# First feed-forward product by Strassen's scheme on pairs of output blocks, in a two-layer hybrid block with a state-space tail

## The chip, the cores and the metric

The kernel is one program on one core of one Trainium2 chip. The time of a run is the device time of that program in microseconds (us); the table below gives the median of three runs. The engines of the core are TensorE (PE in the profile; its weight loads are a row of their own, PEld), VectorE (DVE), ScalarE (ACT), GpSimd (POOL) and SyncE (SP), which only issues transfers here. Each engine works through its own instructions in the order in which the program puts them, and waits where an instruction needs something that another engine has not yet made.

## The reference, cut to what matters

Two hybrid layers run one after the other, then a second block (state space, pooling, gates). The change concerns the feed-forward part of the two layers. There are 512 tokens, the model width D is 1024 and D_FF is 4096:

```
h2 = rmsnorm(x, pre_mlp_g)
ff = jnp.square(jax.nn.relu(h2 @ w_ff1)) @ w_ff2
return x + rmsnorm(ff, post_mlp_g)
```

The product `h2 @ w_ff1` is (512 x 1024) by (1024 x 4096). All matrices are float32. The other products of a layer, the second block and the tables of its state-space branch (`ssm_*` inputs) are computed as before.

## The kernel before

**Tiles.** Activations stand transposed in SBUF: 128 features on the partitions, 512 tokens along the row; a 1024-wide activation is a list of KD = 8 such blocks. A float32 product is made of three products in a shorter format: each operand is split into a high part and a rest (ScalarE casts the high part, VectorE subtracts it), and `mm3` (L77 to L81) issues three matmuls per block: weight high by input high, weight high by input rest, weight rest by input high. All three have their record at L78 or near it, so nearly all of TensorE's work reads as one line.

**Weights.** `load_w` (L167) fetches one 1024 x 128 block of weights into a `raw` tile (512 KB, issued on SP), ScalarE casts it to `wh` (L183), VectorE makes the rest `wl` (L184). Two `raw` buffers are shared by the whole kernel, a third one (`rawx`) takes every third load in the stages that call `third`; `wh` and `wl` have three buffers each, and a cast into one waits until TensorE has used what lay there.

**Products.** `dense` (L194) makes one output block for all 512 tokens: 8 blocks x 3 = 24 matmuls with 512 columns. `dense_half` (L212) does the same for 256 tokens, with 24 matmuls of 256 columns.

**Feed-forward of a layer.** The 32 output blocks of the first product are made in four groups of eight (`gidx`, loop at L1281), and after each group its contribution to the second product is made and added into `acc`. The first six blocks of group 0 are made by halves of the tokens while the normalisation before them still runs (`NFF = 6`); the last two of group 0 and all of groups 1 to 3 use `dense`, which makes 26 such blocks per layer. Each block goes through `relu2`: three ScalarE steps (`ft`, `fq`, cast to `hh`) and one VectorE step (the rest `hl`). In groups 0 to 2 the second product is `dense` too; in group 3 it is `dense_half`, first with weights that are kept in `kw` tiles.

**What else runs there.** `ssm_tables` (L933) is a generator that prepares constant tables for the second block; each `next(tables, None)` lets it make one step, with small VectorE and GpSimd operations (`cmul`, L915 to L921) and a few transposes on TensorE. A half of the tables is made in each layer, inside this feed-forward part, and before the change it is finished before group 3.

**Order.** A scheduler sets the order of instructions on every engine at build time from the order of the code, the buffers and its own estimates; only marked matmuls are kept in program order. Between the engines there are only waits.

Of the kernel before, what the change touches and what calls it, by code (L numbers as in the profile page):

```python
# [9 lines left out]
F32 = mybir.dt.float32  # L10
# [9 lines left out]
P = 128  # L20
SEQ = 512
# [33 lines left out]
def body(  # L55
# [110 lines left out]

    def load_w(src, kn=KD, n=P, pool_h=False, keep=None):  # L167
        turn[0] += 1
        if turn[0] % 3 == 2 and turn[1] is not None and turn[0] > turn[2]:
            raw = turn[1].tile([P, kn, n], F32, tag="rawx", name="rawx", bufs=1)  # L170
        else:
            raw = wp.tile([P, kn, n], F32, tag="raw", name="raw", bufs=2)
# [29 lines left out]

    def dense_q(w, xs, m=P):
# [8 lines left out]
    def dense_half(w, xs, i):  # L212
# [5 lines left out]
        return ps  # L218

# [713 lines left out]
    def ssm_tables(sp, hf):  # L933
        def tl(name, shape=(P, NG)):
            return sp.tile(list(shape), F32, tag=name, name=name)

        prs = slice(NG * hf, NG * hf + NG)
        grs = slice(2 * NG * hf, 2 * NG * hf + 2 * NG)
        lam = {}
        for nm, src in (("lr", ssm_lam_re_2), ("li", ssm_lam_im_2)):  # L940
            row = tl("row" + nm, (NG, P))
# [10 lines left out]
        bre, bim = tl("bre", (P, NG, 16)), tl("bim", (P, NG, 16))  # L952
# [4 lines left out]
        wre, wni = tl("wre", (P, NG, 9, 16)), tl("wni", (P, NG, 9, 16))  # L957
        for dst, src in ((wre, ssm_c_re_2), (wni, ssm_c_im_2)):
            crow = tl("crow", (P, 2, 2, 64))
            for dup in range(2):  # L960
                DMA.dma_start(out=crow[:, :, dup, :], in_=src[0, grs].rearrange("(q g) c p -> (g c) q p", q=2))
            for q in range(2):
                ps = ps_ax((P, 8, 16))
                T.transpose(ps.rearrange("p g c -> p (g c)"), crow[:, q].rearrange("p a b -> p (a b)"), ident)
                for half in range(2):
                    hs = slice(64 * half, 64 * half + 64)
                    V.tensor_copy(out=dst[hs, 4 * q:4 * q + 4, 0, :], in_=ps[hs, half::2, :])
        V.tensor_scalar(out=wni[:, :, 0, :], in0=wni[:, :, 0, :], scalar1=-1.0, scalar2=None, op0=ALU.mult)
# [27 lines left out]
        s16 = (P, NG, 16)  # L996
        tC, tD = tl("tC", s16), tl("tD", s16)
        ebr, ebi = tl("ebr", (P, NG, 8, 16)), tl("ebi", (P, NG, 8, 16))
        cmul(ebr[:, :, 7, :], ebi[:, :, 7, :], bc(cor, s16), bc(coi, s16), bre, bim, tC)
        for j in range(6, -1, -1):  # L1000
            cmul(ebr[:, :, j, :], ebi[:, :, j, :], bc(are, s16), bc(aim, s16), ebr[:, :, j + 1, :], ebi[:, :, j + 1, :], tD, eng=G)
            yield
        for k in range(1, 9):
# [599 lines left out]
```

## Time and profile before

| | us |
|---|---|
| median of 3 runs | 2311.5 |
| lowest and highest of the three | 2302.97, 2313.52 |
| profiled execution: its own time | 2312.67 |
| profiled execution: span of the trace | 2311.0 |
| PE busy | 2247.2 (97%) |
| DVE busy | 1340.0 (58%) |
| ACT busy | 896.2 (39%) |
| POOL busy | 463.2 (20%) |

The trace is of one execution; 1.7 us of that run lie outside its span. Matmuls are pipelined, so a record of one lasts longer than the distance to the next: what a matmul costs in a stretch is the stretch divided by the matmuls that started in it. The feed-forward part of layer 0 lies from about 618 us to 986 us of the span; the 26 blocks of the first product that use `dense`, and the second product of groups 0 to 2, from 656.0 us to 937.4 us.

### The profile page before, as it was taken

How to read it: one execution, taken by the hardware profiler on the slowest of the kernel's cores; microseconds unless marked ns; L12 is line 12 of the kernel's file. 1: busy time of each engine (PE TensorE's matmuls, PEld its weight loads, DVE VectorE, ACT ScalarE, POOL GpSimd, SP SyncE). 2: the span in 40 equal slices, each digit the busy share in tenths (PEclk: the TensorE clock that was granted, in tenths of full speed). 3: DMA queues.
4: the chain of work that ended last, by engine and by line, in shares of the span. 5: the costliest groups of instructions: out<-in, count | busy, mean ns of one | idle time of the engine just before them, and what ended most of it. 6: DMA issues, size and time to landing. Idle time of an engine off the chain costs nothing. (4 is left out here: it accounts for less than half of the span.)

```text
span 2311.0 us, 35255 instructions
## 1 busy us (share of the span) xinstructions
PE 2247.2 (97%) x13596; PEld 1914.8 (83%) x13596; DVE 1340.0 (58%) x2698; ACT 896.2 (39%) x1624; POOL 463.2 (20%) x567
## 2 busy tenths in 40 slices
PE   8999999999999999989999999999999999889998
PEld 7867788888988888988677888789878889878788
DVE  5579793445676333565797934467653335444645
ACT  4454233333443233444533333335432334424333
POOL 1644320200440000246343201004300002100001
PEclk9999999999999999999999999999999999999999
DMA  5223334565434333341234245655343334554344
GB/s 176 62 70 91 87 88 137 157 203 169 145 100 133 95 114 101 109 119 53 71 83 96 85 128 169 196 176 151 83 137 93 112 107 122 162 158 122 109 130 146
DMA packets 463987, 279.98 MB, mean 121 GB/s; under 512 B 48118, under 2 KB 439628, under 8 KB 463308
## 3 DMA queue, kind: packets, MB, share of 16 engines
q1 hardware_dynamic: 462416, 277.54, 41.4%
q8 instruction: 107, 1.75, 0.3%
q14 instruction: 60, 0.49, 0.1%
q10 hardware_dynamic: 1404, 0.19, 0.1%
HBM read 231.57 MB, written 46.11 MB: 120 GB/s over the span
## 5 line engine op out<-in xcount | busy, mean ns | idle before, releaser
L78 PE MATMUL psm<-xsh,wh 128*128 128x512 f32 (+1 forms) x1520 | 595.5, 392 | 1.0 <-ACT xsh L223 1.0
L78 PE MATMUL psm<-xsl,wh 128*128 128x512 f32 (+1 forms) x1520 | 580.9, 382 | 5.5 <-DVE xsl L226 3.9
L78 PE MATMUL psm<-xsh,wl 128*128 128x512 f32 (+1 forms) x1520 | 580.9, 382 | 0.0
L184 DVE TENSOR_TENSOR wl<-raw,wh 128x1024 fp32r<-128x1024 f32 (+2 forms) x249 | 304.0, 1222 | 205.5 <-ACT wh L183 179.6
L183 ACT CAST wh<-raw 128x1024 fp32r<-128x1024 f32 (+2 forms) x196 | 199.2, 1017 | 500.0 <-PE psm L78 448.7
L78 PEld LDWEIGHTS psm<-xsh,wh 128*128 128x128 f32 x1520 | 288.6, 190 | 61.8 <-issue 9.7
L78 PEld LDWEIGHTS psm<-xsl,wh 128*128 128x128 f32 x1520 | 288.8, 190 | 57.9 <-DVE xsl L226 4.6
L78 PEld LDWEIGHTS psm<-xsh,wl 128*128 128x128 f32 x1520 | 288.0, 190 | 56.4 <-issue 0.3
L257 POOL TENSOR_TENSOR sa<-sa,sq 128x256 f32<-128x256 f32 x54 | 52.5, 973 | 821.5 <-ACT sq L252 537.5
L78 PE MATMUL psm<-hh,wl 128*128 128x512 f32 (+1 forms) x480 | 177.5, 370 | 1.4 <-DVE wl L184 1.3
L78 PE MATMUL psm<-hh,wh 128*128 128x512 f32 (+1 forms) x480 | 176.9, 369 | 0.0
L78 PE MATMUL psm<-hl,wh 128*128 128x512 f32 (+1 forms) x480 | 176.6, 368 | 0.0
L183 ACT CAST wh<-rawx 128x1024 fp32r<-128x1024 f32 (+1 forms) x67 | 67.0, 999 | 164.0 <-PE psm L78 151.7
L184 DVE TENSOR_TENSOR wl<-rawx,wh 128x1024 fp32r<-128x1024 f32 (+1 forms) x67 | 77.6, 1158 | 63.1 <-ACT wh L183 60.6
L78 PEld LDWEIGHTS psm<-hh,wl 128*128 128x128 f32 x480 | 90.5, 188 | 18.5 <-DVE wl L184 3.7
L78 PEld LDWEIGHTS psm<-hl,wh 128*128 128x128 f32 x480 | 90.5, 189 | 15.2
L78 PEld LDWEIGHTS psm<-hh,wh 128*128 128x128 f32 x480 | 90.3, 189 | 14.7 <-issue 0.2
L181 POOL TENSOR_SCALAR wh<-raw 128x1024 fp32r<-128x1024 f32 (+1 forms) x53 | 61.5, 1162 | 156.0 <-PE psm L78 124.8
L78 PE MATMUL psm<-ah,wh 128*128 128x512 f32 x256 | 80.7, 396 | 2.9 <-ACT ah L223 2.7
L1310 DVE TENSOR_TENSOR acc<-psm,acc 128x512 f32<-128x512 f32 x32 | 22.1, 692 | 102.2 <-PE psm L78 102.2
L78 PE MATMUL psm<-bh,wh 128*128 128x512 f32 x256 | 80.0, 394 | 0.0
L78 PE MATMUL psm<-kq,xsh 128*128 128x256 f32 x384 | 72.6, 290 | 0.0
(627 smaller groups left out, 4332.6 us busy)
## 6 DMA issues: line engine op xcount, KB each, us to landing
raw<-in_w_in_dram SPq DMA_DIRECT2D x136, 512.0 KB, 3.9
raw<-in_w_ff_dram SPq DMA_DIRECT2D x86, 512.0 KB, 3.9
rawx<-in_w_ff_dram SPq DMA_DIRECT2D x42, 512.0 KB, 4.0
gate<-dg SPq DMA_DIRECT2D x48, 256.0 KB, 3.8
raw<-in_w_up_sw_dram SPq DMA_DIRECT2D x12, 512.0 KB, 5.0
raw<-in_w_up_dn_dram SPq DMA_DIRECT2D x10, 512.0 KB, 4.9
raw<-in_w_o_dram SPq DMA_DIRECT2D x10, 512.0 KB, 3.6
db<-sof SPq DMA_DIRECT2D x16, 256.0 KB, 3.1
```

The source lines that it names most:

```text
L78: return s.issue(nc.tensor.matmul(*a, **k))
L181: G.tensor_scalar(out=h, in0=raw, scalar1=1.0, scalar2=0.0, op0=ALU.mult, op1=ALU.add)
L183: S.copy(out=h, in_=raw)
L184: V.tensor_tensor(out=lo, in0=raw, in1=f32(h), op=ALU.subtract)
L257: (G if s.n in POOL_ACC else V).tensor_tensor(out=s.acc, in0=s.acc, in1=sq, op=ALU.add)
L1310: V.tensor_tensor(out=acc[n], in0=ps, in1=acc[n], op=ALU.add)
```

## The change

The 26 `dense` blocks of the first product in each layer become 13 pairs. A pair is two neighbouring output blocks for all 512 tokens, that is two 1024 x 128 blocks of weights. Inputs (8 blocks), tokens (two halves `p1`, `p2`) and the two output blocks are the three two-fold splits of Strassen's scheme in Winograd's form: seven products of 4 input blocks by 256 tokens instead of eight. A product is 4 x 3 = 12 matmuls of 256 columns, a pair 84 of them; before, two output blocks were 48 matmuls of 512 columns.

What the scheme needs beside the products: `load_pair` makes the sums of weights on GpSimd (four operations of 128 x 512) and splits 3.5 weight blocks instead of 2 into high part and rest. They are called `d` (the block as loaded), `x`, `y` and the half block `z`, whose tiles `s1`, `sh`, `sl` have one buffer each. `fast_pair` puts the seven products into four PSUM tiles (`psa`), and one ScalarE copy and seven VectorE additions of 128 x 256 make the two outputs `y0` and `y1`. `token_sums` makes the sums of inputs once per layer, while the last half-loop of group 0 runs: it reads the normalised input back from memory (eight loads of 256 KB) and holds the results in `ta` and `tb`.

Around it: four raw buffers, two of them in a pool `wx` of the stage (tag `raws`); `rawx` is not used in the stage until group 3's second product; the hidden tiles have 8 buffers instead of 10; `dense2` starts the second product of groups 0 to 2 with two output blocks together, six input blocks each, before it needs the last pair's outputs; the steps of `ssm_tables` stand in another order, share tiles and are finished after the pairs of group 3, so that its tiles, the token sums and `wx` are released there; the `kw` tiles of group 3's second product lie where they were.

```
+    def dense2(ws, xs):
+        ps = [ps_mm() for _ in ws]
+        kn = len(xs)
+        order = (*range(kn - 2), kn - 1, kn - 2)
+        for ks in (order[:-2], order[-2:]):
+            for p, (h, lo) in zip(ps, ws):
+                for k in ks:
+                    mm3(p, h[:, k, :], lo[:, k, :], *xs[k], k == order[0], k == order[-1])
+        return ps
+    def load_pair(src, c, pool):
+        r0, r1 = raw_tile(), raw_tile()
+        for j, r in enumerate((r0, r1)):
+            DMA.dma_start(out=r, in_=src[:, (c + j) * P:(c + j + 1) * P].rearrange("(k p) n -> p k n", p=P))
+        a1, a2 = slice(0, 4), slice(4, 8)
+        s1 = pool.tile([P, 4, P], F32, tag="s1", name="s1", bufs=1)
...
+            S.copy(out=h, in_=raw)
+            V.tensor_tensor(out=lo, in0=raw, in1=f32(h), op=ALU.subtract)
+            return h, lo
+        d = parts(r0)
+        G.tensor_tensor(out=s1, in0=r1[:, a1], in1=r1[:, a2], op=ALU.add)
+        G.tensor_tensor(out=r1[:, a1], in0=r0[:, a1], in1=r1[:, a1], op=ALU.subtract)
+        x = parts(r1)
+        G.tensor_tensor(out=r0[:, a1], in0=s1, in1=r0[:, a1], op=ALU.subtract)
+        G.tensor_tensor(out=r0[:, a2], in0=r0[:, a2], in1=r0[:, a1], op=ALU.subtract)
+        return d, x, parts(r0), parts(s1)
+    def fast_pair(w, xs, ts):
...
+        for b, c, (h, lo), k0, rhs in ((0, p1, d, 0, b11), (0, p2, d, 4, b21), (1, p1, x, 4, t4), (1, p2, x, 0, t3),
+                                       (2, p1, y, 0, t2_), (2, p2, y, 4, b22), (3, p1, z, 0, t1)):
+            for k, ((rh, rl), rc) in enumerate(rhs):
+                mm3(ps[b][:, c], h[:, k0 + k, :], lo[:, k0 + k, :], rh[:, rc], rl[:, rc], k == 0, k == 3, pin=c is p2 and k == 0)
+        y0, y1 = r2("y0", (P, SEQ)), r2("y1", (P, SEQ))
+        u, v = y0[:, p2], y1[:, p2]
+        S.copy(out=u, in_=ps[0][:, p1])
+        for o, i, a in ((y0[:, p1], ps[0][:, p2], u), (u, ps[2][:, p1], u), (v, ps[1][:, p2], u), (y1[:, p1], ps[1][:, p1], v),
+                        (u, ps[2][:, p2], u), (v, ps[3][:, p1], v), (u, ps[3][:, p1], u)):
+            V.tensor_tensor(out=o, in0=i, in1=a, op=ALU.add)
+        return y0, y1
+    def token_sums(st, pool):
...
+            for t, kk in ((a, k), (b, k + 4)):
+                DMA.dma_start(out=t, in_=st.d[:, kk, :])
+                S.activation(out=t, in_=t, func=AF.Copy, scale=pcol(st.gname, st.g0 + kk))
+            V.tensor_tensor(out=a[:, p1], in0=a[:, p2], in1=a[:, p1], op=ALU.subtract)
+            G.tensor_tensor(out=a[:, p2], in0=b[:, p2], in1=a[:, p2], op=ALU.subtract)
+            V.tensor_tensor(out=b[:, p2], in0=b[:, p2], in1=a[:, p1], op=ALU.subtract)
+            V.tensor_tensor(out=b[:, p1], in0=b[:, p1], in1=b[:, p2], op=ALU.subtract)
...
                 while len(hid) < KD:
-                    c0 = (gidx * KD + len(hid)) * P
-                    ps = dense(load_w(w_ff1[l][:, c0:c0 + P]), mid.xs)
-                    next(tables, None)
-                    hid.append(hidden(0))
-                    relu2(ps, *hid[-1])
+                    ys = fast_pair(load_pair(w_ff1[l], gidx * KD + len(hid), spare[0]), mid.xs, ts)
+                    for _ in range(2):
+                        next(tables, None)
+                        hid.append(hidden(0))
+                    for y, hl in zip(ys[::-1], hid[:-3:-1]):
+                        relu2(y, *hl)
...
                 if gidx < 3:
+                    first = dense2([load_w(wsrc(n)) for n in range(2)], hid)
                     for n in range(KD):
-                        ps = dense(load_w(wsrc(n)), hid)
+                        ps = first[n] if n < 2 else dense(load_w(wsrc(n)), hid)
```

Three places show how the instructions of an engine stand. The first is ScalarE where the half-loop of group 0 ends and the first full-width product of the layer begins, in layer 0. Before the change (`ft`, `fq`, `hh` are the last half block's `relu2`, `dt` a step of the tables, `wh_6935` weights of the second product):

```order
L1254 ACTIVATE ft_6711<-psm_6686 128x256
L1256 ACTIVATE fq_6713<-ft_6711 128x256
L223 CAST hh_6498<-fq_6713 128x256
L971 ACT_TABLE_LOAD
L971 ACTIVATE dt_6777<-dt_6777 128x8
L183 CAST wh_6935<-raw_6933 128x1024
L1254 ACTIVATE ft_6813<-psm_6740 128x512
```

The same place in the changed program (`wh_6822` is `x` of the first pair, `sh_6832` its `z`, `wh_6828` its `y`; `psa_6836` holds the pair's first two products, those with `d`):

```order
L1347 ACTIVATE ft_6786<-psm_6761 128x256
L1349 ACTIVATE fq_6788<-ft_6786 128x256
L307 CAST hh_6501<-fq_6788 128x256
L277 COPY y0_6924<-psa_6836 128x256
L1047 ACT_TABLE_LOAD
L1047 ACTIVATE dt_6946<-dt_6946 128x8
L252 CAST sh_6832<-s1_6815 128x512
L252 CAST wh_6822<-raws_6812 128x1024
L252 CAST wh_6828<-raw_6811 128x1024
```

The cast of `x`, which the pair's third product needs, now stands behind the copy of the pair's own first products, and in layer 0 behind the table load as well. In layer 1 the table load and the cast of `z` stand ahead of the copy, and only the copy ahead of `x`:

```order
L252 CAST sh_16985<-s1_16968 128x512
L1047 ACT_TABLE_LOAD
L1047 ACTIVATE dt_17099<-dt_17099 128x8
L277 COPY y0_17077<-psa_16989 128x256
L252 CAST wh_16975<-raw_16965 128x1024
```

The second place is VectorE between the last block of the first product and group 3's second product, layer 0. Before (`kw_8899` is the rest of the first weight block of that product, `hl_8769` the rest of the sixth hidden block):

```order
L184 TENSOR_TENSOR wl_8779<-rawx_8776,wh_8778 128x1024
L226 TENSOR_TENSOR hl_8691<-fq_8694,hh_8690 128x512
L184 TENSOR_TENSOR kw_8899<-rawx_8896,kw_8898 128x1024
L184 TENSOR_TENSOR wl_8818<-raw_8815,wh_8817 128x1024
L226 TENSOR_TENSOR hl_8730<-fq_8733,hh_8729 128x512
L184 TENSOR_TENSOR wl_8857<-raw_8854,wh_8856 128x1024
L184 TENSOR_TENSOR kw_8933<-raw_8930,kw_8932 128x1024
L226 TENSOR_TENSOR hl_8769<-fq_8772,hh_8768 128x512
```

After (`psa_9661` and `psa_9662` hold the last pair's `y` and `z` products):

```order
L280 TENSOR_TENSOR y1_9748<-psa_9660,y1_9748 128x256
L280 TENSOR_TENSOR y0_9747<-psa_9661,y0_9747 128x256
L280 TENSOR_TENSOR y1_9748<-psa_9662,y1_9748 128x256
L280 TENSOR_TENSOR y0_9747<-psa_9662,y0_9747 128x256
L192 TENSOR_TENSOR kw_9786<-raw_9783,kw_9785 128x1024
L192 TENSOR_TENSOR kw_9820<-raw_9817,kw_9819 128x1024
```

The rest of the first kept weights stood four blocks ahead of its use; it now stands behind the last additions of the pairs, and layer 1 has the same order. The third place is VectorE in group 2 of layer 0, between the first pair's weights and the second's (after the change; `A` and `B` are the tables that `cmul` makes, `wl_8472` is `d` of the second pair, `wl_8478` its `x`):

```order
L1002 TENSOR_TENSOR A_8289<-A_8289,tC_7650 128x8x16
L1003 TENSOR_TENSOR tC_7650<-aim_7056,A_8289 128x128
L1001 TENSOR_TENSOR A_8289<-are_7055,A_8289 128x8x16
L1005 TENSOR_TENSOR B_8290<-B_8290,tC_7650 128x8x16
L253 TENSOR_TENSOR wl_8472<-raw_8466,wh_8471 128x1024
L1000 TENSOR_TENSOR tC_7650<-aim_7056,B_8290 128x128
L280 TENSOR_TENSOR y0_8428<-psa_8340,y0_8428 128x256
L1004 TENSOR_TENSOR B_8290<-are_7055,B_8290 128x8x16
```

These 48 `cmul` steps stood among the first `dense` blocks of group 0 and group 1; they now stand among the pairs of group 2, in both layers.

## Rows read from the trace of the kernel before

**Rows 1.** The page's first part: busy us (share of span) x instructions

```profile
PE 2247.2 (97%) x13596; PEld 1914.8 (83%) x13596; DVE 1340.0 (58%) x2698; ACT 896.2 (39%) x1624; POOL 463.2 (20%) x567
```

**Rows 2.** A PE group, 656.0 to 937.44 us: busy, mean ns | idle before, releaser

```profile
L78 PE MATMUL psm<-xsh,wh 128*128 128x512 f32 x208 | 81.8, 393 | 0.0
```

**Rows 3.** Windows: a half-wide stretch, then full-width first product of group 3

```profile
core 0: us, PE busy (x) PEld busy (x) DVE busy (x) ACT busy (x) POOL busy (x), PEclk, DMA share, GB/s
580.04:594.43 14.39, 14.39 (x122) 14.39 (x121) 6.23 (x12) 4.09 (x7) 1.48 (x2) 1.00 0.34 97
893.92:937.44 43.52, 43.52 (x193) 36.04 (x192) 19.63 (x20) 24.43 (x33) 0.00 (x0) 1.00 0.48 137
```

**Rows 4.** ACT groups of the whole span, by shape

```profile
L183 ACT CAST wh<-raw 128x1024 fp32r<-128x1024 f32 x179 | 187.9, 1050 | 476.9 <-PE psm L78 438.2 <-issue 13.5 <-DVE wl L184 8.8
L1256 ACT ACTIVATE fq<-ft 128x512 f32<-128x512 f32 x52 | 32.9, 632 | 1.4
L223 ACT CAST hh<-fq 128x512 fp32r<-128x512 f32 x52 | 32.2, 620 | 1.6
L1254 ACT ACTIVATE ft<-psm 128x512 f32<-128x512 f32 x52 | 30.7, 591 | 0.0
...
L859 ACT COPY sc<-psa 128x256 f32<-128x256 f32 x48 | 15.3, 371 | 13.3 <-PE psa L78 13.0
```

**Rows 5.** DVE groups of the whole span, by shape

```profile
L184 DVE TENSOR_TENSOR wl<-rawx,wh 128x1024 fp32r<-128x1024 f32 x59 | 72.1, 1221 | 62.4 <-ACT wh L183 60.0 <-PE psm L78 2.4
...
L226 DVE TENSOR_TENSOR hl<-fq,hh 128x512 fp32r<-128x512 f32 x52 | 36.0, 692 | 20.4 <-ACT hh L223 20.4
...
L1324 DVE TENSOR_TENSOR acc<-psm,acc 128x256 f32<-128x256 f32 x32 | 13.3, 421 | 34.6 <-PE psm L78 34.6
...
L921 DVE TENSOR_TENSOR wni<-wni,tC 128x128 f32<-128x128 f32 x16 | 4.9, 308 | 0.1
```

**Rows 6.** POOL groups of the whole span, two inputs, 128x512

```profile
L545 POOL TENSOR_TENSOR tg<-tri,gh 128x512 fp32r<-128x512 f32 x16 | 21.2, 1325 | 6.5 <-ACT gh L487 3.6 <-PE psa L78 2.9
...
L722 POOL TENSOR_TENSOR st<-st,eg 128x512 f32<-128x512 f32 x8 | 8.3, 1040 | 61.8 <-DVE st L747 43.1 <-DVE st L745 18.7
```

**Rows 7.** PE in order of time, end of group 3's first product: start, us

```profile
937.22 0.39 PE L78 MATMUL psm<-xsh,wl 128*128 128x512 f32 x1
937.44 0.28 PE L78 MATMUL psm<-hh,kw 128*128 128x256 f32 x1
```

**Rows 8.** Line 971 on ACT: duration ns min/median/max

```profile
L971 ACT ACT_TABLE_LOAD  x2: 1283/1283/1283, 659.3 to 1642.8; - x2
L971 ACT ACTIVATE dt<-dt x2: 208/208/209, 663.5 to 1644.1; 128x8 f32<-128x8 f32 x2
```

**Rows 9.** Transfers: KB each, median us from issue to landing

```profile
raw<-in_w_ff_dram SPq DMA_DIRECT2D x86, 512.0 KB, 3.9
```

**Rows 10.** PE in order of time, two pauses: start, us [idle before <- releaser]

```profile
530.76 0.80 PE L78 MATMUL psm<-ah,wh 128*128 128x512 f32 x1 [2.01 <-ACT ah L223]
...
992.39 0.39 PE L78 MATMUL psm<-wh,xsl 128*128 128x272 f32 x1 [1.97 <-DVE xsl L226]
```

**Rows 11.** Windows behind these pauses, and one at 1974 us (columns as Rows 3)

```profile
530.80:534.20 3.40, 3.40 (x8) 2.42 (x8) 3.09 (x5) 1.90 (x2) 0.00 (x0) 0.50 0.92 286
1974.60:1978.00 3.40, 3.40 (x18) 3.40 (x18) 1.91 (x4) 1.04 (x1) 0.71 (x1) 0.50 1.07 416
993.00:1009.00 16.00, 15.73 (x129) 15.39 (x128) 10.46 (x19) 7.99 (x18) 7.59 (x10) 1.00 0.64 196
```

**Rows 12.** Window: the second half-loop of group 0, layer 0 (columns as Rows 3)

```profile
638.60:656.00 17.40, 16.29 (x133) 15.82 (x133) 9.04 (x18) 11.71 (x26) 2.96 (x5) 1.00 0.46 135
```

**Rows 13.** DVE in order of time, among the tables of layer 0: start, us

```profile
681.96 0.28 DVE L918 TENSOR_TENSOR wre<-wre,tC 128x128 f32<-128x128 f32 x1
682.16 0.37 DVE L919 TENSOR_TENSOR tR<-pi,rotr 128x8 f32<-128x8 f32 x1
682.45 1.21 DVE L184 TENSOR_TENSOR wl<-rawx,wh 128x1024 fp32r<-128x1024 f32 x1
```

More of the change, by code (lines that the diff above doesn't have):

```diff
@@ L165, in third, with raw_tile @@
         turn[1:] = pool, turn[0] + SKIP
+    spare, raws = [None], [0]
+    def raw_tile():
+        raws[0] += 1
+        if spare[0] is not None and raws[0] % 4 < 2:
+            return spare[0].tile([P, KD, P], F32, tag="raws", name="raws", bufs=2)
+        return wp.tile([P, KD, P], F32, tag="raw", name="raw", bufs=2)
     def load_w(src, kn=KD, n=P, pool_h=False, keep=None):
@@ L171, in load_w @@
         else:
-            raw = wp.tile([P, kn, n], F32, tag="raw", name="raw", bufs=2)
+            raw = raw_tile() if kn == KD and n == P else wp.tile([P, kn, n], F32, tag="raw", name="raw", bufs=2)
         DMA.dma_start(out=raw, in_=src.rearrange("(k p) n -> p k n", p=P))
@@ new lines, in token_sums @@
+    def token_sums(st, pool):
+        p1, p2 = slice(0, HS), slice(HS, SEQ)
+        ts = []
+        for k in range(4):
+            a, b = r2("tsa", (P, SEQ)), r2("tsb", (P, SEQ))
+            for t, kk in ((a, k), (b, k + 4)):
[5 more added lines that the diff above has]
+            V.tensor_tensor(out=b[:, p1], in0=b[:, p1], in1=b[:, p2], op=ALU.subtract)
+            t = []
+            for nm, src in (("ta", a), ("tb", b)):
+                hl = [pool.tile([P, SEQ], F32R, tag=f"{nm}{k}{j}", name=nm) for j in range(2)]
+                split(*hl, src)
+                t.append(hl)
+            ts.append(t)
+            yield ts
@@ L956, in ssm_tables @@
                               in_=src[0, grs].rearrange("(i two) p c -> two p i c", two=2)[half])
[L957 to L968, printed above, removed]
         yield
@@ L994, in ssm_tables @@
         yield
[L996 to L1003, printed above, removed]
-            cmul(wre[:, :, k, :], wni[:, :, k, :], bc(are, s16), bc(aim, s16), wre[:, :, k - 1, :], wni[:, :, k - 1, :], tC, conj=True)
-            yield
-        DMA.dma_start(out=d_w[0][:, prs], in_=wre[:, :, 1:9, :])
-        DMA.dma_start(out=d_w[1][:, prs], in_=wni[:, :, 1:9, :])
-        rot = tl("rotr", (P, NG, 64)), tl("roti", (P, NG, 64))
+        ra = sp.tile([P, NG * 9 * 16], F32, tag="A", name="rot")
+        rot = [ra[:, 512 * i:512 * i + 512].rearrange("p (i b) -> p i b", i=NG) for i in range(2)]
         pa, pb = (tl("pr"), tl("pi")), (tl("qr"), tl("qi"))
@@ L1030, in ssm_tables @@
             DMA.dma_start(out=d_r[i][:, prs], in_=rot[i])
+        yield
+        s16 = (P, NG, 16)
+        tC, tD = tl("tC", s16), tl("tD", s16)
+        ebr, ebi = big("A", 8), big("B", 8)
+        cmul(ebr[:, :, 7, :], ebi[:, :, 7, :], bc(cor, s16), bc(coi, s16), bre, bim, tC)
+        for j in range(6, -1, -1):
+            cmul(ebr[:, :, j, :], ebi[:, :, j, :], bc(are, s16), bc(aim, s16), ebr[:, :, j + 1, :], ebi[:, :, j + 1, :], tD, eng=G)
+            yield
         for i, src in enumerate((ebr, ebi)):
```

77 lines of the change are left out of this document (59 added, 18 removed).

## Prediction

> **What bounds the kernel now.** I read the page's engine shares first: TensorE is busy 97% of the span, VectorE 58%, ScalarE 39%, GpSimd 20% [rows 1]. An engine that is never idle can only be helped by giving it less to do, and everything else here counts only where it makes TensorE wait. Second, TensorE's groups in the changed stretch of layer 0: the 26 dense blocks of the first product show as 208 matmuls for each of three kinds, 8 per block, with no idle time ahead of them [rows 2]. A record lasts 0.39 us, but matmuls overlap, so the price is read from windows: 192 matmuls with 512 columns start in 43.52 us, 0.2267 us each, and a half-wide stretch of five blocks, 120 matmuls with 256 columns and two others, takes 14.39 us, at most 0.120 us each [rows 3]. The half-wide stretch is not quite half the price, and there the weight loads are busy all 14.39 us, against 36.04 of 43.52 us in the full-width one: a half-wide matmul is held by its weight load. Third, who waits: ScalarE's weight casts were idle 476.9 us before them, 438.2 of it for TensorE to release a buffer [rows 4]. The weights stand ready early, and the stage is bound by TensorE alone.
>
> **What TensorE saves.** A pair was 48 x 0.2267 = 10.88 us and becomes 84 x 0.120 = 10.08 us, 0.80 us less. That it saves 7% and not the eighth that seven products for eight suggest is the weight load. Two layers have 26 pairs: **20.8 us** less. The gain is gone if a half-wide matmul takes 10.88 / 84 = 0.1295 us.
>
> On this price the notes differ. The Trainium skill, "TensorE: Matmul & The Clock Gate", section "Back-to-back issue gap", says that a stream of weight loads and matmuls is spaced by both together, and gives 131 ns at 512 columns and 81 ns at 128. On a line between them 256 columns would take some 98 ns (an estimate from that page); a pair would be 6.3 us before and 8.2 after, and the change would cost 50 us. The trace disagrees at 512 columns by a factor (227 ns) and at 256 (120 ns), and the measurement decides; that both operations set the spacing agrees with the busy weight loads above.
>
> **What a pair asks of the others.** VectorE: 3 rests of 1.22, a half one of 0.69, seven additions of 0.42, two hidden rests of 0.69, that is 8.7 us [rows 5]. ScalarE: 3 casts of 1.05, a half one of 0.62, the copy of 0.37, two times 0.59 + 0.63 + 0.62, that is 7.8 us [rows 4]. GpSimd: the trace has no such sums of weights; the nearest rows with two inputs and 128 x 512 take 1.04 and 1.33 us, so four are 4.2 to 5.3 us [rows 6]. All are below 10.08 us, so in the steady state TensorE covers them, and I cost them at nothing there. VectorE is the nearest (86%); what that cover is worth is the second rival.
>
> **First pair of a layer.** Call the start of its first matmul T. The two products with `d` (24 matmuls) end at T + 2.88, with 0.16 more for the last one's record (0.28 long, spaced 0.12) [rows 7]. The scheduler put `x`'s cast behind the copy of just these products. In layer 0 ScalarE does the copy to T + 3.41, the table load (1.28) to 4.69, the exponential (0.21) to 4.90 [rows 8], `z`'s cast to 5.52 and `x`'s cast to 6.57; VectorE's rest ends at 7.79. TensorE can do two matmuls on the high part and wants the rest at 3.12: it stands 4.7 us. In layer 1 only the copy is ahead: 3.41, 4.46, 5.68, a stand of 2.6 us. Together **+7.2 us**. Nothing else comes last: a transfer of weights lands 3.9 us after its issue [rows 9], and `x`'s block goes when the buffer's former tenant is released, one block (2.88 us) before T, so it lands at T + 1.0; two sums on GpSimd end at 3.1 to 3.7, before ScalarE is free for the cast. Bounds: 0, if the weights' cast runs before the copy, as a different start of T could allow only for `z`, and 10, if GpSimd is slower under this load.
>
> **Into group 3's second product.** Before, TensorE goes from one to the other with no gap: the starts are 0.22 us apart [rows 7]. Now the rest of the first kept weights stands on VectorE behind the last pair's last two additions, which need the last product: 0.16 + 0.42 + 0.42 + 1.22 less two overlaps of 0.08 = 2.06 us after it, wanted at 0.24. A gap of 1.8 us in each layer, **+3.6 us**; bounds 0 and 6. From the last pair of groups 0 to 2 into their second product `dense2` does two blocks' first six inputs ahead, 36 full-width matmuls or 8.2 us, and the last pair's additions and `relu2` (0.84 + 2 x 1.84 + 0.69, about 5.4 us) fit in it: nothing.
>
> **Clock.** Behind a pause of 2.01 us the rows show TensorE at its lower level, granted 0.50 for 3.40 us, and there is a second such stretch at 1974 us; behind a pause of 1.97 us it stayed at 1.00 [rows 10, 11]. In the first of them 8 full-width matmuls took 3.40 us, against 1.81 at full clock: 1.6 us lost. The stands of 4.7 and 2.6 us are longer than the pause of 2.01, the two gaps of 1.8 shorter than 1.97, so I count two falls, **+3.2 us**, with bounds of none and four (6.4).
>
> **Token sums.** The half-loop in which they are made, 17.4 us, already holds 11.71 us of ScalarE and 9.04 of VectorE [rows 12]. The sums add 16 scalings on ScalarE (0.62, 9.9 us) and, on VectorE, 12 operations of 0.42 and 8 of 0.69 (10.6 us): ScalarE has 4.2 us too much, VectorE 2.3. Most of this slides into the first pair, where `t4`, `t3` and the rest are wanted only from the third product on, and where I have already counted a stand that covers it. Take **+2.0 us** for both layers; bounds 0 and 8.4. The eight loads are issued on SP ahead of later weights, which have a buffer more than before.
>
> **Tables.** 48 `cmul` steps of 0.31 us moved from groups 0 and 1 to VectorE's row among the pairs of group 2. From the second weights of that group to the rest of the fourth pair's `z` VectorE has 48 x 0.31 + 9 x 1.22 + 3 x 0.69 + 19 x 0.42 + 4 x 0.69 + 5 x 0.22 = 39.7 us of work, from 2.4 us after the group's first matmul to 42.1; wanted it is at 3 x 10.08 + 8.88 = 39.1. That is up to 3.0 us late, in each layer. But starts there are 0.20 and 0.29 us apart where the records last 0.28 and 0.37 [rows 13]: 0.08 less for each of some 80 operations, enough for no delay at all. Take **+1.6 us** for both; bounds 0 and 6.
>
> **Sum.** 2312.7 - 20.8 + 7.2 + 3.6 + 3.2 + 2.0 + 1.6 = 2309.5 us against the profiled execution's own 2312.67 us, which is 1.2 above the median of 2311.5; beside that median it would be 2308.3. I write 2309. About 0.5%, 11.6 us, is what a measurement here can tell from no change, so faster begins below 2300 and slower above 2323.
>
> **Rivals.** First, the transitions hide: TensorE's gain stays whole, since the real order of events at the first pair and at group 3 is a little earlier than I make it. 2312.7 - 20.8 = 2292 us with nothing lost, 2296 with the gap of group 3 alone. For it: weights are early everywhere in the kernel before [rows 4]. Against it: the instruction orders of both places are fixed, and a gap follows from each by adding known durations.
>
> Second, and on the other side, **VectorE becomes the bound** of a pair. It works in order, and it now holds weight rests, which must be early, and additions that wait for a product, which are late; behind a waiting addition everything queues. The cycle is 8.7 us plus the waits W that no other work fills. It decides from W = 2.2 us, where the pair is back at 10.88 us. With W = 2.9 a pair is 11.6: 26 x 0.72 = 18.7 us lost in place of 20.8 gained, and with the other terms (7.2 + 3.6 + 3.2) 2345 us; with W = 2.2 2327. For it: VectorE's rests already waited 60 us for casts [rows 5], and tables, additions and rests now share one row. Against it: four raw buffers and three sets of `wh` let the rests run a product ahead, and W would need two whole hand-overs of a pair unfilled.
>
> Third, the product doesn't get cheaper: a half-wide matmul is held by its weight load, and with sums, casts and copies about, it spaces as in the half-loop of group 0, 133 matmuls in 17.40 us or 0.131 each [rows 12], pauses included. A pair is then 11.0 us, 26 pairs cost 2.8 us more, and the sum gives 2312.7 + 2.8 + 17.6 = 2333 us. Against it: that stretch has 1.1 us of idle TensorE, without which it is 0.122. The Trainium skill's page above ("Back-to-back issue gap") has its dearer half-wide product in this direction.
>
> **How the numbers follow.** Forecast (sum above): chance 0.66; with its bounds it goes from 2298 to 2322, of which I put 0.06 below 2300, 0.55 in the middle and 0.05 above 2323. First rival: 0.18, faster. Second: 0.13, slower. Third: 0.03, slower. So faster 0.24, same 0.55, slower 0.21. The range of 8 in 10 takes the forecast's span, half of the first rival (from 2294), the third and the nearer half of the second (2327 to 2333): 2294 to 2333, which leaves out some 0.16.
>
> **What would show it.** Right: half-wide matmuls at 0.12 us within a pair of groups 1 and 2 and 40.3 us for four of them; one stand of about 4.7 us on TensorE behind the 24th matmul of the first pair, released by VectorE's rest of `x`, and one of 2.6 in layer 1, each with 0.50 granted behind it; a gap of 1.8 us before the kept weights. Wrong: TensorE idle in every pair with VectorE's rests as releaser (second rival), no idle time anywhere (first), or 0.13 us between matmuls without idle time (third). What would make the whole working wrong is a stand at a place that I cost at nothing, such as `dense2` or the pairs among the tables.

## The result: 1.5% slower

The changed kernel takes 2345.8 us (median of four runs, 2339.8 to 2347.8) against 2312.5 us of the kernel before in the same comparison: a ratio of 1.0148, 95% interval 1.0114 to 1.0182. That lies above the stated range (2294 to 2333). The profiled execution has a span of 2346.1 us, 35.1 us more than before.

The page of the changed kernel, busy time by engine (answers [rows 1]):

```profile
PE 2241.6 (96%) x14532; PEld 1953.5 (83%) x14532; DVE 1517.7 (65%) x2976; ACT 955.5 (41%) x1734; POOL 629.1 (27%) x683
```

Windows over the four pairs of group 3, layer 0 and layer 1 (columns as in [rows 3]; the answer to its second window):

```profile
914.04:954.44 40.40, 40.31 (x337) 40.11 (x335) 32.28 (x44) 24.34 (x36) 16.26 (x10) 1.00 0.31 90
1906.92:1947.33 40.41, 40.32 (x337) 40.11 (x335) 32.77 (x44) 24.38 (x36) 15.34 (x10) 1.00 0.31 91
```

Four pairs take 40.40 us where eight dense blocks took 43.52: 0.78 us less for a pair, and TensorE hardly stands there (busy 40.31 us). The saving of the scheme is real, and 26 x 0.78 = 20.3 us. It is paid back elsewhere. What TensorE waited for in the changed kernel (engine and what it ran <- for whom: us in total, times, longest; the first rows and those of the feed-forward part):

```profile
PE psa L78 <- ACT wh L252: 20.7, 4, 9.7
...
PE psa L78 <- DVE wl L253: 6.1, 8, 1.5
...
PE psa L81 <- DMA crow<-in_ssm_c_im_dram: 5.4, 2, 2.8
...
PE psm L78 <- DVE kw L192: 4.8, 2, 2.4
...
PE psa L78 <- DVE y L280: 3.7, 4, 1.5
```

Both layers are in each row. By place, both layers together: 17.3 us at the first pair (forecast 7.2), 8.7 in group 1 and 5.2 in group 2 (1.6 for the tables, which were to be late in group 2 only), 5.4 at two transposes of a table (`crow`, nothing), 5.9 at group 3's second product (3.6). With the saving that is -20.3 + 42.5, less the 1.3 us of such stands before. That leaves 14 us of the 35.1, and the clock can hold them: the mean granted clock is 0.983 against 0.991, that is (0.017 x 2346 - 0.009 x 2311) x 2 = 38 us more at half clock (the lower level, granted 0.50), in which at most half the time is lost. In the feed-forward parts alone the lower level makes up about (0.04 x 334 + 0.03 x 336) x 2 = 47 us, where before it was not granted there at all. Windows over these parts, changed kernel and kernel before, layer 0 and layer 1 of each (columns as in [rows 3]):

```profile
656.00:990.00 334.00, 310.92 (x1981) 281.63 (x1980) 232.09 (x445) 138.12 (x201) 108.44 (x105) 0.96 0.36 102
1649.00:1985.00 336.00, 316.46 (x2036) 287.41 (x2035) 236.81 (x458) 142.70 (x211) 111.64 (x113) 0.97 0.37 105
...
656.00:990.00 334.00, 331.81 (x1682) 281.27 (x1681) 164.25 (x354) 123.47 (x180) 37.54 (x64) 1.00 0.37 105
1636.00:1972.00 336.00, 331.92 (x1681) 281.00 (x1679) 166.27 (x356) 123.49 (x179) 38.68 (x63) 1.00 0.37 107
```

**The first pair, layer 0.** ScalarE of the changed kernel in order of time (start, us, [idle before <- releaser]):

```profile
659.18 0.36 ACT L277 COPY y<-psa 128x256 f32<-128x256 f32 x1
663.62 1.28 ACT L1047 ACT_TABLE_LOAD   x1 [4.08 <-DMA dt<-in_ssm_log_dt_dram]
666.90 0.21 ACT L1047 ACTIVATE dt<-dt 128x8 f32<-128x8 f32 x1 [2.00 <-DMA dt<-in_ssm_log_dt_dram]
667.02 0.60 ACT L252 CAST sh<-s 128x512 fp32r<-128x512 f32 x1
667.52 1.04 ACT L252 CAST wh<-raws 128x1024 fp32r<-128x1024 f32 x1
```

And TensorE over the same stretch:

```profile
658.68 0.28 PE L78 MATMUL psa<-xsh,wl 128*128 128x256 f32 x1
668.62 0.79 PE L78 MATMUL psa<-tb,wh 128*128 128x256 f32 x2 [9.66 <-ACT wh L252]
669.88 0.58 PE L78 MATMUL psa<-tb,wl 128*128 128x256 f32 x1 [0.47 <-DVE wl L253]
```

The order is the one that was read beforehand, copy, table load, exponential, `z`, `x`. But the table load and the exponential wait 6.1 us for `dt`, a small transfer whose issue starts at 654.52 us and for which ScalarE waits until 666.90 us. The matmuls behind the stand are at the lower clock (granted 0.50 from 668.62 to 672.00 us, and the matmuls are spaced 0.21 us).

**Group 1, layer 0.** GpSimd of the changed kernel in order of time:

```profile
742.52 0.73 POOL L1003 TENSOR_TENSOR tD<-aim,A 128x128 f32<-128x128 f32 x1
743.22 0.40 POOL L1001 TENSOR_TENSOR A<-are,A 128x128 f32<-128x128 f32 x1
743.59 1.52 POOL L1005 TENSOR_TENSOR B<-B,tD 128x128 f32<-128x128 f32 x1
745.18 0.79 POOL L1000 TENSOR_TENSOR tD<-aim,B 128x128 f32<-128x128 f32 x1
745.94 0.40 POOL L1004 TENSOR_TENSOR B<-are,B 128x128 f32<-128x128 f32 x1
746.30 1.28 POOL L257 TENSOR_TENSOR s<-raw 128x512 f32<-128x512 f32 x1
747.54 0.47 POOL L1002 TENSOR_TENSOR A<-A,tD 128x128 f32<-128x128 f32 x1
747.97 1.26 POOL L258 TENSOR_TENSOR raw<-raws,raw 128x512 f32<-128x512 f32 x1
```

A window there, all engines (columns as in [rows 3]):

```profile
740.00:750.00 10.00, 7.72 (x63) 7.31 (x61) 5.16 (x7) 5.62 (x10) 9.84 (x14) 1.00 0.18 52
```

GpSimd works 9.84 of 10 us (29.45 of the 30 from 730 to 760 us), and the sums of a pair's weights (L257, L258) stand between steps of the tables (L1000 to L1005). Each layer has 42 such steps on GpSimd; the forecast counted the tables' steps on VectorE alone.

**What GpSimd does to VectorE.** DVE groups of the changed kernel, 914.0 to 957.4 us, group 3's pairs (busy, mean ns of one | idle before, releaser; they answer [rows 5]):

```profile
L280 DVE TENSOR_TENSOR y<-psa,y 128x256 f32<-128x256 f32 x28 | 10.8, 416 | 0.1
L253 DVE TENSOR_TENSOR wl<-raws,wh 128x1024 fp32r<-128x1024 f32 x5 | 8.4, 1683 | 3.4 <-ACT wh L252 3.4
L253 DVE TENSOR_TENSOR wl<-raw,wh 128x1024 fp32r<-128x1024 f32 x5 | 7.5, 1505 | 2.2 <-ACT wh L252 2.2
L310 DVE TENSOR_TENSOR hl<-fq,hh 128x512 fp32r<-128x512 f32 x6 | 6.4, 1069 | 2.2 <-ACT hh L307 2.2
```

The additions, which read one input from PSUM, take the 0.42 us of before. The rests, with both inputs in SBUF, take 1.68 and 1.50 us in place of 1.22, and 1.07 in place of 0.69. Of the 16 sums that four pairs need, GpSimd makes 10 in this window; the others were made ahead. Which of the rests are long is seen in order of time, VectorE at layer 1's first pair:

```profile
1652.93 1.82 DVE L310 TENSOR_TENSOR tb<-tsb,tb 128x512 fp32r<-128x512 f32 x1
1654.67 1.48 DVE L295 TENSOR_TENSOR tsb<-tsb 128x256 f32<-128x256 f32 x1
...
1658.09 0.68 DVE L310 TENSOR_TENSOR tb<-tsb,tb 128x512 fp32r<-128x512 f32 x1
1658.72 0.41 DVE L310 TENSOR_TENSOR hl<-fq,hh 128x256 fp32r<-128x256 f32 x1
```

GpSimd at the same time:

```profile
1652.91 1.28 POOL L258 TENSOR_TENSOR raw<-raw 128x512 f32<-128x512 f32 x1
1654.28 1.60 POOL L260 TENSOR_TENSOR raw<-s,raw 128x512 f32<-128x512 f32 x1
1655.95 1.33 POOL L261 TENSOR_TENSOR raw<-raw 128x512 f32<-128x512 f32 x1
```

The same rest of 128 x 512 takes 1.82 us while GpSimd makes a sum and 0.68 after its last sum (which ends at 1657.28). The last token sum is held up so (1.48 us at 1654.67), then ScalarE's cast of it, and behind that on ScalarE the cast of `x`: the stand of 6.68 us in layer 1 starts with this and not with the copy. About half of layer 1's stand hangs on it: with the sums off GpSimd (run 12) 3.6 of 7.1 us are left.

### The profile page after: what moved, and what is told of

Same layout as the page of the kernel before. It is cut to its first block, busy times and chain, and to the rows that moved or that the text cites. A ratio compares the mean times of both kernels' runs of the same rounds, so it can differ in the third digit from the quotient of the medians.

```text
span 2346.1 us, 37815 instructions
## 1 busy us (share of the span) xinstructions
PE 2241.6 (96%) x14532; PEld 1953.5 (83%) x14532; DVE 1517.7 (65%) x2976; ACT 955.5 (41%) x1734; POOL 629.1 (27%) x683
## 5 line engine op out<-in xcount | busy, mean ns | idle before, releaser
L78 PE MATMUL psm<-xsh,wh 128*128 128x512 f32 (+1 forms) x1104 | 431.9, 392 | 1.4 <-ACT xsh L307 1.0
L78 PE MATMUL psm<-xsl,wh 128*128 128x512 f32 (+1 forms) x1104 | 418.7, 379 | 4.3 <-DVE xsl L310 3.9
L78 PE MATMUL psm<-xsh,wl 128*128 128x512 f32 (+1 forms) x1104 | 419.0, 380 | 0.0
L78 PEld LDWEIGHTS psm<-xsh,wh 128*128 128x128 f32 x1104 | 210.3, 191 | 44.5 <-issue 7.6
L78 PEld LDWEIGHTS psm<-xsl,wh 128*128 128x128 f32 x1104 | 210.9, 191 | 40.3 <-DVE xsl L310 4.6
L78 PEld LDWEIGHTS psm<-xsh,wl 128*128 128x128 f32 x1104 | 210.1, 190 | 40.0 <-issue 0.3
L78 PE MATMUL psa<-tb,wh 128*128 128x256 f32 x416 | 82.2, 295 | 25.0 <-ACT wh L252 20.7
L78 PE MATMUL psa<-xsh,wh 128*128 128x256 f32 x312 | 89.1, 286 | 0.0
L78 PE MATMUL psa<-xsl,wh 128*128 128x256 f32 x312 | 88.9, 285 | 0.0
L78 PE MATMUL psa<-xsh,wl 128*128 128x256 f32 x312 | 88.9, 285 | 0.0
```

What stands on the lines that cost most here:

```text
L78: return s.issue(nc.tensor.matmul(*a, **k))
```

## The experiments

The theory after the result had two causes: **tables queued ahead** of the pairs' own work on the engines' in-order rows, and **GpSimd's sums**, which make VectorE wait. The rivals were that VectorE's own row is the bound of a pair (the second rival of the prediction), and that the rest of the change (tiles, buffers) costs by itself. Times are medians; the ratio is to the kernel before on the same chip.

| run | us | ratio (95%) |
|---|---|---|
| changed kernel | 2345.8 | 1.0148 (1.0114 to 1.0182) |
| 1 no pair in group 0 | 2336.7 | 1.0122 (1.0097 to 1.0147) |
| 2 table steps asked for later | 2346.3 | 1.0161 (1.0136 to 1.0186) |
| 3 no Strassen | 2330.1 | 1.0086 (1.0060 to 1.0113) |
| 4 kept weights last | 2351.6 | 1.0183 (1.0157 to 1.0209) |
| 5 tables held back | 2319.2 | 1.0032 (1.0020 to 1.0044) |
| 6 as 5, no pair in group 0 | 2306.9 | 0.9980 (0.9972 to 0.9989) |
| 7 as 6, kept weights last | 2309.0 | 0.9999 (0.9987 to 1.0011) |
| 8 as 6, last two blocks dense | 2307.1 | 0.9988 (0.9977 to 0.9998) |
| 9 no Strassen, tables held back | 2313.4 | 1.0008 (0.9998 to 1.0018) |
| 10 as 6, sums on VectorE | 2301.9 | 0.9964 (0.9951 to 0.9977) |
| 11 as 5, sums on VectorE | 2302.0 | 0.9959 (0.9943 to 0.9974) |
| 12 changed kernel, sums on VectorE | 2318.7 | 1.0030 (1.0019 to 1.0041) |

**Run 1, no pair in group 0.**

```
+                    if gidx == 0:
+                        c0 = len(hid) * P
+                        ps = dense(load_w(w_ff1[l][:, c0:c0 + P]), mid.xs)
+                        next(tables, None)
+                        hid.append(hidden(0))
+                        relu2(ps, *hid[-1])
+                        continue
                     ys = fast_pair(load_pair(w_ff1[l], gidx * KD + len(hid), spare[0]), mid.xs, ts)
```

> The last two blocks of group 0 are plain dense blocks again, in both layers; pairs stay in groups 1 to 3 (24 of 26). Theory (the loss is a set of separate stands, each with its own cause): the two stands at the first pair go, 9.66 + 0.47 us in layer 0 and 6.68 + 0.46 us in layer 1 by the trace of the changed kernel, and with them the stretches at half clock behind them, worth some 6 us; two pairs' saving of 0.78 us each is lost. 2345.8 - 17.3 - 6 + 1.6 = about 2324 us. Rival (VectorE's in-order row is the bound of every pair, and the first stand only its start): the lateness shows up at the next pairs, and the time stays above 2338 us.

2336.7 us: 9 us less and not 22, and the intervals of the two ratios overlap. TensorE stands again, at the next thing. TensorE in order of time, layer 0 and layer 1:

```profile
668.96 0.80 PE L78 MATMUL psm<-xsh,wh 128*128 128x512 f32 x1 [6.28 <-ACT wh L191]
...
1656.13 0.24 PE L81 MATMUL psa<-ident,row 8*128 8x8 f32 x1 [5.77 <-DMA row<-in_ssm_lam_im_dram]
```

SyncE's issues ahead of the first of these:

```profile
654.67 6.86 SPq L1043 DMA_DIRECT2D lbi<-in_ssm_b_im_dram  x2
661.63 2.70 SPq L181 DMA_DIRECT2D raws<-in_w_ff_dram  x2
```

What waits (`psm<-xsh,wh`) is the last block of group 0, the second that is dense again. SyncE sits 6.9 us in the issue of a table's two transfers, and the weights are issued behind it. Neither the theory nor the rival had this place. SyncE's is one more row on which the tables stand ahead. In the kernel before the same issue also takes 7.0 us (from 653.88 us), but there TensorE does not stand behind it.

**Run 2, table steps asked for later.** The two `next(tables, None)` of a pair move to the blocks of the second product, two for each.

> The pairs let the tables make no step; each block of the second product of groups 0 to 2 lets them make two. Theory (table steps on GpSimd and VectorE hold up the sums and rests of the pairs, and two transposes of the tables wait for a transfer): the stands in groups 1 and 2 go (8.7 us for weights and outputs in group 1, 5.2 in group 2, 5.4 for crow, both layers together) with some 5 us of half clock, and the wait of ScalarE for dt in the first pair of layer 0, about 4 us: 2345.8 - 28 = about 2318 us. Rival (GpSimd's sums and VectorE's additions are late by themselves, without the tables): the stands in groups 1 and 2 stay, and only crow and dt go, 2345.8 - 10 = about 2336 us.

No change: 2346.3 us. The edit did not do what it was for, except at `crow`: those stands (5.4 us) are gone, while the stands in group 1 grow from 8.7 to 12.4 us. The scheduler still puts the table steps between the sums on GpSimd and the wait for `dt` ahead of the first pair's `x` (a stand of 11.16 us there), since it orders by its own estimates. So the run does not decide between the two sides.

**Run 3, no Strassen.**

```
-                        sums, ts = token_sums(mid, tpool), None
+                        sums, ts = iter(()), None
...
-                    ys = fast_pair(load_pair(w_ff1[l], gidx * KD + len(hid), spare[0]), mid.xs, ts)
+                    ys = [dense(load_w(w_ff1[l][:, c0 * P:c0 * P + P]), mid.xs) for c0 in range(gidx * KD + len(hid), gidx * KD + len(hid) + 2)]
```

> Each pair is two dense blocks again and the token sums are left out; the raw buffers, the order and place of the tables, eight hidden tiles, dense2 and the release of the tiles ahead of group 3's second product stay as in the changed kernel. Theory: nearly all of the loss comes from what the pairs ask of the other engines; without them only the wait for crow (5.4 us) and a smaller gap ahead of the kept weights are left: 2312.5 + 4 to + 10, 2317 to 2323 us. Rival (the moved tables and released tiles are what costs): 2330 us or more.

2330.1 us, the rival's number: some 20 us of cost are there without any pair. Its profile shows where, TensorE in order of time in layer 1:

```profile
1643.55 0.20 PE L81 MATMUL psa<-ident,row 8*128 8x8 f32 x1 [1.58 <-DMA row<-in_ssm_lam_re_dram]
1644.36 0.79 PE L78 MATMUL psm<-xsh,wh 128*128 128x512 f32 x1 [0.62 <-ACT wh L191]
...
1651.56 0.24 PE L81 MATMUL psa<-ident,row 8*128 8x8 f32 x1 [5.98 <-DMA row<-in_ssm_lam_im_dram]
```

The two transfers share one `row` tile now, so the second is issued only behind the first's transpose (at 1643.77 us), and TensorE has it 7.8 us later. TensorE's row has the first transpose ahead of the first dense block and the second behind two of its matmuls. In layer 0 the second transfer also stands behind SyncE's 6.77 us of issue, and TensorE waits 2.69 us for it.

**Run 4, kept weights last.** Group 3's second product starts with blocks 5 and 6, together on the first six inputs; the kept blocks follow.

> Group 3's second product begins with its three blocks whose weights are not kept, two of them together on the first six inputs; the five kept ones come behind. Theory (the gap there is the rest of the first kept weights behind the last additions): the gaps of 2.42 and 2.35 us, the 1.15 us behind the first and two stretches at half clock go: 2345.8 - 5.9 - 2 = about 2338 us. Rival (the outputs of the last pair are late anyway, as the next wait): a gap of 2 us or more stays there, and the time stays at 2344 us or more.

The gap at the kept weights goes, and others come: in layer 0 TensorE waits 2.03 us for the last hidden tile and 1.4 us in smaller pieces. The rival holds. Whether the run is slower than the changed kernel is not shown, since the intervals overlap; layer 1's first pair, far from the edit, stands 10.56 us in it and not 6.68. **Run 7** put three blocks ahead, on top of run 6, and gained nothing; in layer 1 TensorE waits 4.15 us there for a hidden tile:

> As the run before it in this list, and group 3's second product begins with its three blocks whose weights aren't kept, all three together on the first six inputs (6.5 us of TensorE ahead of the last pair's outputs, where two blocks gave 4.3 and left 3.5 us of waits). Theory: the gap of 2.4 us in each layer falls below 1: about 3 us below that run, 2300 us, which is 9 us below the kernel before. Rival: the outputs of the last pair take over as the wait, no gain.

**Run 5, tables held back.** Each step's instructions are tied, engine by engine, behind the block of the second product after which the code asks for it; a transpose comes one step behind its transfer. `refs` holds each engine's last instruction of a weight load or a matmul, on GpSimd the last sum; `issue_after` sets an order on an engine and adds no wait between engines. The call in the pairs is dropped.

```
+    def behind(gen):
+        with ExitStack() as q:
+            for i in list(refs.values()):
+                q.enter_context(tc.issue_after(i.ins))
+            next(gen, None)
...
-                        next(tables, None)
+                        behind(tables)
+                        behind(tables)
```

> The changed kernel with one thing different: every step of the tables is tied, on each engine, behind the instructions of the second-product block after which the code asks for it, so that no table step can slip ahead into the pairs on GpSimd, or ahead of the first pair's casts on ScalarE and SyncE; transposes of a table's transfer come one step behind the transfer. Theory (tables queued ahead of the pairs' own work): the stands in groups 1 and 2 (13.9 us in both layers) and at crow (5.4) go, the first pair's 17.3 us fall to some 8, and 6 us of half clock go: 2345.8 - 13 - 5.4 - 9 - 6 = about 2312 us. Rival (the pairs are held up by their own work, VectorE and GpSimd without tables): stands of 10 us or more stay in groups 1 and 2, 2328 us or more.

2319.2 us, 27 us less (2312 expected; the rival's bound was 2328). The stands at `crow` and in group 2 are gone, group 1 keeps 3.2 and 3.5 us. The first pair keeps more than thought; TensorE in order of time, layer 0:

```profile
663.03 0.54 PE L81 MATMUL psa<-tb,wh 128*128 128x256 f32 x2 [2.56 <-ACT wh L255]
667.38 0.58 PE L81 MATMUL psa<-tb,wl 128*128 128x256 f32 x1 [3.82 <-DVE wl L256]
```

Nothing of the tables is ahead of it now; VectorE's row in this stretch has three rests of 128 x 256 at some 1.5 us each (0.41 alone) while GpSimd makes the four sums. **Run 9** repeats run 3 with the tables held back:

> Two dense blocks for every pair and no token sums, as in the earlier run without Strassen's scheme, which took 2330 us, and now with the table steps tied behind the second product's blocks. Theory (that run's 20 us over the kernel before are the tables' transfers and transposes queued ahead of the layer's first full-width blocks): 2312 us, within 4 us of the kernel before. Rival (fewer hidden tiles, raw buffers from another pool or dense2 cost something by themselves): 2320 us or more.

2313.4 us, within the interval of no change: run 3's 20 us were the tables' places; tiles, buffers and `dense2` cost nothing that shows.

**Run 6, as run 5 and no pair in group 0.**

> As the run with the tables held back, and the last two blocks of group 0 are dense blocks, so that 24 pairs are left. Theory: the first pair's stand (8 us expected to be left) and its half clock go, two pairs' saving of 1.6 us goes: about 9 us below the run with the tables held back alone, 2303 us. Rival (the token sums and the weights' sums are late for whatever pair comes first): the stand moves to group 1 and the time stays within 3 us of that run.

2306.9 us, 12 less than run 5 (9 expected). For the first time the kernel is faster than before, by 0.2%, with 24 pairs. **Run 8** also makes the last two blocks of group 3 dense:

> As the run with the tables held back and no pair in group 0, and the last pair of group 3 is two dense blocks too, so that 22 pairs are left. Theory (the gap of 2.4 us ahead of the kept weights, and the half clock behind it, come from the last pair's additions, which stand ahead of the first kept rest on VectorE): in each layer 2.36 us of gap and some 1.5 of half clock go and 0.78 of saving goes: 6 us below that run's 2306.9, 2301 us. Rival (dense blocks bring the same wait for their own last outputs): 2306 us or more.

The gap of 2.36 us becomes one of 1.00 in layer 0 (with 0.65 more behind it) and goes in layer 1, yet the time does not move. By these stands 3 us go and 1.6 us of saving go too, and the rest is within the intervals. That more half clock would go with it was not borne out: the granted clock, averaged over all executions, is 0.989 in both runs.

**Run 10, as run 6 and the sums of weights on VectorE.** All four operations of `load_pair` change their engine; the first:

```
- G.tensor_tensor(out=s1, in0=r1[:, a1], in1=r1[:, a2], op=ALU.add)
+ V.tensor_tensor(out=s1, in0=r1[:, a1], in1=r1[:, a2], op=ALU.add)
```

> As the run with the tables held back and no pair in group 0, with the four sums of weights per pair made on VectorE in place of GpSimd. VectorE then has 8.7 + 4 x 0.69 = 11.4 us a pair, less 0.08 us of overlap for each of its 17 operations, 10.1 us, against TensorE's 10.08; GpSimd has nothing. Theory (what slows VectorE is that its operations with both inputs in SBUF wait while a GpSimd operation runs: 0.41 us became 1.5): without GpSimd's operations these go back to 0.41 and 0.69 us, and the pairs stay near 10.1 us: 2305 to 2315 us. Rival (VectorE's in-order row is the bound as soon as its own work reaches TensorE's, and waits come on top): each of 24 pairs 1.3 us longer, 2335 us or more.

2301.9 us, less than the 2305 to 2315 expected. VectorE has four operations more for each pair, and the kernel is no slower for it: the ratio is 0.9964 against run 6's 0.9980, with intervals that just overlap. DVE groups of this run over group 3's pairs, 890.0 to 933.0 us:

```profile
L283 DVE TENSOR_TENSOR y<-psa,y 128x256 f32<-128x256 f32 x28 | 10.8, 416 | 3.0 <-PE psa L81 2.9
...
L256 DVE TENSOR_TENSOR wl<-raws,wh 128x1024 fp32r<-128x1024 f32 x5 | 6.1, 1220 | 0.2 <-ACT wh L255 0.2
L313 DVE TENSOR_TENSOR hl<-fq,hh 128x512 fp32r<-128x512 f32 x6 | 4.1, 686 | 2.1 <-ACT hh L310 2.1
...
L263 DVE TENSOR_TENSOR raw<-s,raw 128x512 f32<-128x512 f32 x2 | 1.4, 681 | 0.0
```

The rests are back at 1.22 and 0.69 us, the sum takes 0.68. VectorE's row as the bound of a pair is refuted: with more in it the pairs are hardly late (stands of at most 0.25 us in groups 1 and 2).

**Run 11, as run 5 and the sums on VectorE (all 26 pairs), and run 12, the changed kernel with this one edit.**

> All 26 pairs, the tables held back, the sums of weights on VectorE: it differs from the run with the tables held back alone (2319 us) by the engine of the sums. Theory (the stands of 6.4 and 7.0 us that this run still had at the first pair come from GpSimd's sums, which make VectorE's rests and token sums wait): at most 3 us of stand are left in each layer, 2300 to 2306 us. Rival (the first pair is late because its weights and the token sums come late, on whatever engine): 5 us or more of stand in each layer, 2311 us or more.

> The changed kernel with one thing different: the four sums of weights per pair on VectorE. The tables stand where the change put them. Theory (two causes that add: GpSimd's sums, and the tables queued ahead): the stands of group 1 (8.7 us in both layers) go with 3 us of half clock, and part of layer 1's first pair (3 us); the wait for dt, the tables' transfers on SyncE and crow stay: about 2330 us. Rival (VectorE has no room for the sums beside the tables): 2343 us or more.

Run 11: 2302.0 us, 17 us less than run 5, and 4.0 and 4.4 us of stand left at the first pairs, between the two bounds. A sum also takes less time on VectorE (0.68 us against about 1.3), so the gain could come from earlier sums and not from the end of the waiting. At layer 0's first pair the two runs decide that. In both TensorE has finished the products with `d` at 660.47 us. ScalarE's cast and VectorE's rest of `x`, first in run 5, then in run 11:

```profile
661.93 1.04 ACT L255 CAST wh<-raws 128x1024 fp32r<-128x1024 f32 x1 [0.27 <-POOL raws L261]
666.12 1.21 DVE L256 TENSOR_TENSOR wl<-raws,wh 128x1024 fp32r<-128x1024 f32 x1
...
662.87 1.05 ACT L255 CAST wh<-raws 128x1024 fp32r<-128x1024 f32 x1 [0.32 <-DVE raws L261]
663.95 1.22 DVE L256 TENSOR_TENSOR wl<-raws,wh 128x1024 fp32r<-128x1024 f32 x1
```

The sum, and with it the cast, is 0.9 us later in run 11, and the rest is 2.2 us earlier, since VectorE's row ahead of it is no longer held up. At the other pairs the two effects are not told apart.

Run 12: 2318.7 us, 27 us less than the changed kernel, where 16 were expected. In its profile group 1 has no stand left, the first pair of layer 1 3.6 us in place of 7.1, group 3's second product 2.6 in place of 3.6 in layer 0; layer 0's first pair (9.67) and `crow` (2.70 and 2.59) stay as the theory says. So removing either cause alone is worth 27 us and removing both 44 (2345.8 to 2302.0). They overlap by 10 us, as is to be expected where the tables' steps stand between the sums.

Runs 10 and 11 take less time than both kernels, 0.4% less than the one before (intervals 0.9951 to 0.9977 and 0.9943 to 0.9974). Run 11's trace still has 14.1 us of stands in the feed-forward parts, so that -20.3 + 14.1 - 1.3 gives -7.5 us; the medians differ by 9.3.

## Why the prediction was wrong, step by step

- **TensorE's saving**, 20.8 us forecast, 20.3 measured: right, and the half-wide matmul is spaced 0.12 us. The third rival falls with it.
- **"All are below 10.08 us, so ... TensorE covers them, and I cost them at nothing there"** is the step that failed first. The sums of weights were priced by two rows of GpSimd [rows 6], and as GpSimd's own time. Two things were missing. GpSimd's row also holds the tables' 42 steps a layer, and VectorE's operations with both inputs in SBUF took up to 1.1 us longer beside GpSimd's. For a pair these are 4.35 + 1.38 = 5.7 us of VectorE and, by the row of 1.3 us, 5.2 of GpSimd. If they run one after the other, that is 10.9 us, above TensorE's 10.08 (an estimate from these rows). In group 3 it is covered by weights made ahead (10 sums of 16 in the window); in group 1, where the tables' steps are in the rows too, it isn't. Moving the sums away is worth 27 us from the changed kernel (run 12).
- **The first pair**, 7.2 us forecast, 17.3 measured. In layer 0 the term that was mis-sized is the table load and exponential, 1.5 us by their durations. [rows 8] has their starts too, 659.3 and 663.5 us: 4.2 apart where the load lasts 1.28. The 2.9 us between are a wait for `dt`, which cost nothing before and could be read there. In layer 1 the copy was taken for the cause, and the token sums, which were to slide behind a stand already counted, came ahead of it in ScalarE's row, held up by GpSimd; of 7.1 us half goes with GpSimd's sums (run 12). "Nothing else comes last" priced the end of GpSimd's sums, not what they hold up.
- **Tables**, 1.6 us forecast and the term with the largest miss. Of VectorE's 48 steps the estimate was for group 2 only, where 5.2 us were lost; GpSimd's steps in group 1 (8.7), `crow` (5.4) and the transfers on SyncE were not in it, though the change put them among the pairs or ahead of them. Holding all back is worth 27 us (run 5); without pairs their places cost 17 (run 3 to run 9).
- **Into group 3's second product**: the mechanism was right (2.42 and 2.35 us at the kept rest, 1.8 each forecast), and the other orders of runs 4, 7 and 8 made nothing cheaper.
- **Clock**: two falls forecast, 3.2 us; what is left of the difference is some 14 us, with 0.96 and 0.97 granted over the feed-forward parts. There were more stands and longer ones. The length of a stand alone, by which the falls were counted, did not decide: behind `crow`'s 2.78 us in layer 0 the granted clock was 0.83 over the next 10 us, behind its 2.61 us in layer 1 it stayed at 1.00.
- **The second rival** gave 2345 us, and 2345.8 was measured, but the agreement is of numbers. Its mechanism, VectorE's own work in order, is refuted by runs 10 and 11, in which VectorE has more to do, and already by the 40.40 us of group 3's four pairs, for each of which it asked 11.6 us. The forecast's nothing for the way into the second products of groups 0 to 2 was right: no stand stood out there. Two slips in the sums decide nothing: 0.84 + 2 x 1.84 + 0.69 is 5.2 and not 5.4, and all terms at their upper bounds give 2329 us, not the 2322 at which the forecast's span ends.

What stays open: 4.0 and 4.4 us at the first pairs of run 11, whose token sums and weights come late on whatever engine, how the 14 us at the lower clock divide among the stands, and why SyncE sits 7 us in one issue.

## What to carry to other kernels

When a change takes work off a saturated engine and gives it to idle ones, add up each of the others' rows with everything that stands in them there, in order, transfers and side work included; a busy share of 20% (27% after the change) says nothing about a row that is full for 30 us. Price the helpers together: where two engines hold each other up, add their operations as one budget. And read starts as well as durations: a gap between two neighbours on an idle engine is a wait that starts to cost when something is queued behind it.

## What the runs showed of the hardware

VectorE and GpSimd hold each other up: a subtraction of 128 x 256 with both inputs in SBUF took 0.41 us alone and about 1.5 while GpSimd ran sums, one of 128 x 512 0.68 and 1.82, while all 182 additions with an input from PSUM took 0.41 to 0.43 us. It goes both ways, GpSimd's sums took 1.29 us alone and 2.16 next to a rest (group 3, 939.6 us). The Trainium skill says so in "SBUF — State Buffer", section "SBUF: two separate sides": GpSimd and VectorE share a pair of ports under an exclusive lock, held for a whole instruction, by a VectorE operation with two SBUF inputs against a GpSimd operation that reads SBUF. The trace agrees: the longer rests last up to 1.1 us more, where a sum takes 1.3, and the additions from PSUM are free of it. By that rule the prediction would have had 10.9 us per pair on one resource (the estimate above).

A transfer of little data can be slow: `dt`, 128 rows of 8 numbers in two parts, was issued at 654.52 us and waited for until 666.9, 12 us, where 512 KB of weights land in 3.9 [rows 9].
